# A hybrid decoder layer on one core: the gate projected as [token, channel] blocks and applied before the transposes

## The chip, the cores and the metric

One core of a Trainium2 chip runs the whole layer as one program. The metric is the device time of one execution in microseconds (us); three executions of the kernel before took 892.24, 895.63 and 896.28 us, median 895.63.

## What is computed

One decoder layer over 256 tokens of width 2048, all in float32:

```python
h    = rms_norm(x, norm_g)
proj = h @ dn_w_in                       # q 1536 | k 1536 | v 3072 | a, b 48 | xq 1024 | z 4096
mix  = deltanet_branch(...)              # causal conv + SiLU, 24 value heads of 128, gated delta rule,
                                         # each head's output through rms_norm with out_g
xa   = memory_cross_attention(xq, ...)   # 4 heads of 256 channels against 256 memory tokens
y    = concatenate([mix, xa]) * silu(z)  # 4096 channels
out  = x + y @ w_out
```

The gate is `silu(z)`, and z takes 4096 of the 11,312 columns of the input projection. The delta rule needs, for each of 24 heads and 2 chunks of 128 tokens, the inverse of a unit lower triangular 128 x 128 matrix.

## The kernel before, in words

**Weights.** All weights come as 272 units of [128, 1024] words, in the order of the list `STREAM`. `wnext` (lines 226 to 252) loads a unit on the SP queue into `st` (5 buffers), lets ScalarE cast it to a high part (line 244) and VectorE subtract for the low part (line 246); both lie in `wt` (4 buffers). Every product is three matmuls: high x high, high x low, low x high. All matmuls go through line 162 and all transposes through line 166, ordinary operations of ScalarE, VectorE and POOL through line 94; so the tiles' names tell them apart. `hkt` holds the normalised tokens, 16 tiles of [128 channels, 256 tokens], high and low.

**Two kinds of projection.** `proj_a` (lines 265 to 278) makes a tile of 128 channels x 256 tokens. The weight is stationary. For each of 16 steps there are two matmuls into one PSUM bank `pa`: the weight's high part against both parts of the tokens (512 columns), and its low part against the tokens' high part (256 columns), which is added to the second half. `halves` then adds the two halves: a ScalarE copy and a VectorE add. q, k, v, xq and z are made so. `proj_b` (lines 299 to 321) makes two tiles of 128 tokens x 512 channels at once, in two banks: tokens stationary, weights moving, three matmuls of 512 columns for each step and token half. The memory's keys and values ("K", "V") and the output projection ("o") are made so, banks by tag "A" or "pa", two of each.

**The order.** A loop at the end of `hybrid_kernel` takes one unit after another of `STREAM`: V, K and the decay inputs, 8 xq tiles, k tiles 0 to 5 with z tiles 24 to 31 between them, z tiles 0 to 11, and then twelve rounds of q, v, v, where the first two rounds also hold the other k tiles and the first six hold two z tiles each; at last the output blocks. Between units it runs side processes (generators) that are due by a cost model: `conv`, `gram`, `inverse`, `merge`, `delta`, `attend`, `decay`, `split_y`. The framework then orders instructions for each engine and sets the waits.

**The gate.** z tile pairs become `zs` [channel, token] (`silu`, 32 times 256 columns). In `delta` the output `o` [token, channel] is scaled by its norm on ScalarE (line 1054), transposed (`poT`, line 1061) and multiplied by `zs` on VectorE (line 1064). The cross-attention makes `xaT` [channel, token] directly and `gate_xa` multiplies. `split_y`, from round 9 on, splits each product into `yhi` and `ylo`, the stationary operands of the output projection.

**The inverses.** `inverse(g)`, for 12 of 24 heads each, solves the 32 x 32 diagonal blocks of 24 matrices on VectorE. It writes them transposed into the diagonal of full 128 x 128 matrices in DRAM (`dY`) and untransposed, compactly, into `dX`, both on ScalarE's queue. Then, three times, six loads fetch pieces of `dX` into `XN` and two loads fetch whole rows of `dY` into two tiles `Y`, zeros included; `merge` joins the blocks with small matmuls (`pm`). `zero_scratch` (line 787) writes the zeros of both `dY` once, on the SP queue.

Of the kernel before, what the change touches and what calls it, by code (L numbers as in the profile page):

```python
# [48 lines left out]
STREAM = [("V", 0)] * 8 + [("V", 1)] * 8 + [("K", 0)] * 8 + [("ab", 0)] + [("K", 1)] * 8  # L49


def _tiles(*ts):
    for t in ts:
        STREAM.extend([t, t])


for _t in range(8):
    _tiles(("x", _t))
for _t in range(6):
    _tiles(("k", _t), ("z", 24 + _t))  # L60
_tiles(("z", 30), ("z", 31))
for _t in range(12):
    _tiles(("z", _t))
for _t in range(NPAIR):
    _tiles(("q", _t), ("v", 2 * _t), ("v", 2 * _t + 1))
    if _t < 2:
        _tiles(*[("k", _k) for _k in ((6, 7, 8), (9, 10, 11))[_t]])
    for _i in (2 * _t + 12, 2 * _t + 13):
        if _i < 24:
            _tiles(("z", _i))  # L70
for _t in range(4):
    STREAM.extend([("o", _t)] * 16)


@with_exitstack
def hybrid_kernel(ctx: ExitStack, tc: tile.TileContext, x, xT, memT, W, prm_d, cst_d, out):
# [144 lines left out]
    wpos = [0]  # L221
# [4 lines left out]
    def wnext():  # L226
        st = stp.tile([128, 1024], F32, name="st", tag="st")
        wt = wp.tile([128, 2, 1024], F32R, name="wt", tag="wt")
        hi, lo, src = wt[:, 0, :], wt[:, 1, :], st
        if STREAM[wpos[0]][0] == "ab":  # L230

            v = wt.rearrange("p a (k c) -> p (a k c)", c=64).rearrange("p (k a c) -> p k a c", a=2, c=64)
            hi, lo, src = v[:, :, 0, :], v[:, :, 1, :], st.rearrange("p (k c) -> p k c", c=64)
        parts = 2 if wpos[0] == 0 else 1
        dma[0] = max(dma[0], free.pop(0)) + 1.46
        for a in range(parts):
            w = slice(a * 1024 // parts, (a + 1) * 1024 // parts)
            sy.dma_start(st[:, w], W[wpos[0]][:, w])
# [12 lines left out]
        free.append(ve.end)  # L251
        ahead.append((wt, ve.end))

    def wload():

        while wpos[0] < W.shape[0] and len(ahead) <= LOOK:
            wnext()
        wt, t = ahead.pop(0)
        now[0] = max(now[0], t)
        return wt  # L260
# [38 lines left out]
    def proj_b(steps, act, tag, done, before=None):  # L299
# [3 lines left out]
        for s in range(0, n, 2):  # L303
# [321 lines left out]
    xaT = [None] * 4  # L625
# [28 lines left out]
    def attend(hd, qh, ql, sq):  # L654
# [41 lines left out]
        for dt in range(2):  # L696
            c0 = (hd % 2) * 256 + dt * 128
            for m in range(2):
                exact(px[:, dt * 256 : (dt + 1) * 256], [t[:, c0 : c0 + 128] for t in vm[m][hd // 2]],
                      [t[:, m * 256 : (m + 1) * 256] for t in (pTh, pTl)], start=(m == 0), stop=(m == 1))  # L700
        yield 0.2
        xa = S2("xaT", [2, 256])
        se.copy(xa.rearrange("p a t -> p (a t)"), px)
        yield
        xaT[hd] = xa
# [70 lines left out]
    dY = [dp.tile([24, 129 * C], F32, name=f"dY{g}", tag=f"dY{g}") for g in range(2)]  # L776
# [9 lines left out]

    def zero_scratch():
        z = S2("zero", [512])
        po.memset(z, 0.0)
        for g in range(2):  # L790
            sy.dma_start(dY[g].rearrange("s e -> (s e)").rearrange("(p a e) -> p a e", p=128, a=12),
                         z[:, 0:258].unsqueeze(1).to_broadcast([128, 12, 258]))
            yield 8.0

    def inverse(g):
# [33 lines left out]
        for f in range(2):  # L829
            se.dma_start(diag(dY[g])[:, 16 * f : 16 * f + 16], xt[f])  # L830
# [3 lines left out]
        nat = dX[g].rearrange("(s k) r c -> k r s c", k=4)  # L834
        for q in range(3):
# [7 lines left out]
            ys = []  # L843
            for p2 in range(2):
                y = S2("Y", [4, C])
                s0 = 8 * q + 4 * p2
                se.dma_start(y, mat(dY[g])[s0 : s0 + 4].rearrange("s r c -> r s c"))
                ys.append(y)
            yield
            yield from merge(6 * g + 2 * q, xs, ys)  # L850
# [58 lines left out]
    zs = [None] * 16  # L909

    def z_done(j, i):
        def done(pt):
            if i == 0:
                zs[j] = S2("zs", [2, 256])
            spawn(silu(pt, j, i), 0.2)
        return done

    def silu(pt, j, i):
# [3 lines left out]
        ready.add(f"z{j}{i}")  # L922
# [3 lines left out]
    def split_y():  # L926
        for j in [12, 13, 14, 15] + list(range(NPAIR)):
            yield from until(lambda: yf[j] is not None)
            yield from calm()
            yhi[j], lo = S2("yhi", [2, 256], F32R), S2("ylo", [2, 256], F32R)  # L930
            se.copy(yhi[j], yf[j])
            yield
            ve.tensor_tensor(out=lo, in0=yf[j], in1=yhi[j], op=ALU.subtract)
            ylo[j] = lo

    def gate_xa(hd):
        yield from until(lambda: {f"z{12 + hd}0", f"z{12 + hd}1"} <= ready and xaT[hd] is not None)
        z = zs[12 + hd]
        ve.tensor_tensor(out=z, in0=xaT[hd], in1=z, op=ALU.mult)
        yf[12 + hd] = z  # L940
# [18 lines left out]
    def delta(p):  # L959
# [86 lines left out]
        yield  # L1046
        ve.scalar_tensor_tensor(out=e4[:, 1], in0=e4[:, 0], scalar=1.0 / 128,
# [7 lines left out]
        yield from pe_soon()  # L1055
        yield from until(lambda: {f"z{p}0", f"z{p}1"} <= ready)
        pt = PS("m", "poT")
        for h in range(2):
            for b in range(NB):
                w = (2 * h + b) * C  # L1060
# [31 lines left out]
    def process(kind, t):  # L1092
# [13 lines left out]
        if kind == "z":  # L1106
            return proj_a(z_done(t // 2, t % 2))
# [98 lines left out]
```

## Time and profile before

| | |
|---|---|
| profiled execution | 892.58 us, its span 890.8 us |
| TensorE matmuls, busy | 870.6 us (98%), 5331 instructions |
| VectorE, ScalarE busy | 643.3 us (72%), 565.9 us (64%) |
| DMA | 171.5 MB, mean 192 GB/s |
| mean granted TensorE clock | 0.992 of 2.4 GHz |

Times in all rows are microseconds from the span's start, unless marked ns. PE is TensorE's matmuls, PEld its weight loads, DVE VectorE, ACT ScalarE, SP the sync engine; "SPq" and "ACTq" are DMA issues on these engines' queues. A busy TensorE is not TensorE at its peak: a matmul's shown duration overlaps the next one's, so the spacing of matmuls is read from long gapless pieces.

### The profile page before, as it was taken

The page shows a single profiled execution, that of the slowest core. Times are in us where ns is not written, and L with a number is a line of the kernel's source. Part 1 is how long each engine was busy: PE and PEld are TensorE (multiplying, and loading weights), DVE is VectorE, ACT ScalarE, POOL GpSimd, SP SyncE. Part 2 cuts the span into 40 slices and gives each one's busy share as a digit, 9 for nine tenths or more (in the row PEclk, how much of TensorE's full clock was granted, in tenths as well). Part 3 has the DMA queues.
Part 4 walks back from the last instruction along what each step waited for, and adds up shares of the span by engine and source line. Part 5 has one row for each costly group of instructions (what it writes and reads, how often), then busy time and mean ns, then how long its engine had stood idle before and what let it go on. Part 6 is the DMA issues. An engine that isn't in the chain of part 4 may idle for free.

```text
span 890.8 us, 14438 instructions
## 1 busy us (share of the span) xinstructions
PE 870.6 (98%) x5331; PEld 743.9 (84%) x5331; DVE 643.3 (72%) x1267; ACT 565.9 (64%) x1046; POOL 41.9 (5%) x51
## 2 busy tenths in 40 slices
PE   7998989999999999999999999999999999999998
PEld 5886879888888888878888888888888888888886
DVE  7778777678968799867687879895688655554442
ACT  8655365587768787457667977656688656433341
POOL 0000000001000000210100000010000000000000
PEclk9998999999999999999999999999999999999999
DMA  8963885556777765776465554466354544756560
GB/s 289 346 208 124 196 269 141 166 171 216 241 207 236 232 225 173 223 205 186 153 189 189 189 187 147 148 206 201 121 178 154 170 158 159 257 192 223 192 210 24
DMA packets 82351, 171.46 MB, mean 192 GB/s; under 512 B 23760, under 2 KB 39912, under 8 KB 82280
## 3 DMA queue, kind: packets, MB, share of 16 engines
q1 hardware_dynamic: 51344, 161.25, 56.1%
q10 hardware_dynamic: 30936, 9.28, 4.3%
q8 instruction: 42, 0.69, 0.3%
q14 instruction: 29, 0.24, 0.1%
HBM read 160.50 MB, written 10.01 MB: 191 GB/s over the span
## 4 chain that ended last, share of the span: by engine, by line
PE 79%; DMA 8%; DVE 5%; issue 4%; ACT 3%; POOL 1%; ACTq 0%; SPq 0%; POOLq 0%; DVEq 0%
PE pa L162 44%; PE pb L162 26%; DMA st<-W_d 3%; PE pO L162 2%; DVE wt L246 2%; DMA dX<-inN 1%; PE pm L162 1%; DMA Y<-dY 1%; ACT wt L244 1%; PE pU L162 1%; DMA inN<-dN 1%; PE pkq L162 1%; PE xsc L162 1%; PE xo L162 1%; DVE acc L94 1%
## 5 line engine op out<-in xcount | busy, mean ns | idle before, releaser
L162 PE MATMUL pa<-hkt,wt 128*128 128x512 f32 (+1 forms) x2816 | 517.8, 341 | 3.9 <-ACT wt L244 2.0
L162 PEld LDWEIGHTS pa<-hkt,wt 128*128 128x128 f32 x2816 | 431.3, 189 | 63.4 <-DVE wt L246 2.4
L246 DVE TENSOR_TENSOR wt<-st,wt 128x1024 fp32r<-128x1024 f32 (+1 forms) x274 | 332.5, 1216 | 126.6 <-ACT wt L244 121.7
L244 ACT CAST wt<-st 128x1024 fp32r<-128x1024 f32 (+1 forms) x274 | 284.9, 1046 | 151.4 <-PE pb L162 91.3
L162 PE MATMUL pb<-wt,yhi 128*128 128x512 f32 x512 | 159.4, 392 | 0.0
L162 PEld LDWEIGHTS pb<-wt,yhi 128*128 128x128 f32 x512 | 94.8, 188 | 19.2 <-ACT yhi L94 0.3
L162 PE MATMUL pb<-wt,ylo 128*128 128x512 f32 x256 | 99.8, 390 | 0.0
L162 PE MATMUL pb<-wt,mkt 128*128 128x512 f32 x384 | 93.1, 401 | 3.6 <-ACT wt L244 2.3
L162 PEld LDWEIGHTS pb<-wt,mkt 128*128 128x128 f32 x384 | 73.7, 194 | 21.1 <-ACT wt L244 2.7
L94 DVE SCALAR_TENSOR_TENSOR acc<-raw,prm,acc 128x255 f32<-128x255 f32 x144 | 68.8, 478 | 16.2 <-ACT acc L94 15.0
L94 ACT ACT_TABLE_LOAD x43 | 55.2, 1283 | 3.3 <-DVE acc L94 1.9
L162 PEld LDWEIGHTS pb<-wt,ylo 128*128 128x128 f32 x256 | 48.1, 188 | 10.1
L94 ACT COPY raw<-pa 128x256 f32<-128x256 f32 x48 | 17.8, 372 | 29.4 <-PE pa L162 18.3
L94 DVE TENSOR_TENSOR inT<-inXT,inN 96x1 f32<-96x1 f32 (+22 forms) x92 | 29.5, 340 | 1.6 <-DMA inN<-dN 1.3
L94 ACT ACTIVATE acc<-raw,prm 128x256 f32<-128x256 f32 x48 | 24.4, 509 | 8.5 <-DMA XN<-dX 4.3
L94 DVE TENSOR_SCALAR dec<-erow,gcc 128x128 f32<-128x128 f32 x96 | 24.5, 284 | 7.2 <-DMA erow<-dgc 7.1
L94 DVE TENSOR_REDUCE inXT<-inT 96x1 f32<-96x1 f32 (+22 forms) x92 | 28.6, 335 | 0.4
L94 POOL TENSOR_TENSOR e<-e,mhalf 128x4 f32<-128x4 f32 x12 | 15.3, 1279 | 286.9 <-DVE e L94 286.9
L94 DVE TENSOR_TENSOR raw<-pa,raw 128x256 f32<-128x256 f32 x48 | 20.1, 419 | 12.0 <-ACT raw L94 11.9
L94 ACT COPY zs<-pa 128x256 f32<-128x256 f32 x32 | 11.8, 369 | 23.9 <-PE pa L162 23.9
L94 POOL TENSOR_TENSOR srk<-skt,mhalf 128x2 f32<-128x2 f32 x12 | 12.9, 1076 | 230.5 <-DVE skt L94 216.5
L94 ACT ACTIVATE o<-o,e 128x128 f32<-128x128 f32 x48 | 16.1, 395 | 5.7 <-POOL e L94 5.6
(196 smaller groups left out, 697.2 us busy)
## 6 DMA issues: line engine op xcount, KB each, us to landing
st<-W_d SPq DMA_DIRECT2D x272, 512.0 KB, 4.1
erow<-dgc SPq DMA_DIRECT2D x24, 256.0 KB, 5.0
dY<-zero SPq DMA_DIRECT2D x2, 1548.0 KB, 11.0
dN<-dec ACTq DMA_DIRECT2D x12, 256.0 KB, 2.7
Y<-dY ACTq DMA_DIRECT2D x12, 256.0 KB, 4.0
xraw<-xT_d SPq DMA_DIRECT2D x8, 256.0 KB, 5.7
res<-x_d SPq DMA_DIRECT2D x8, 256.0 KB, 4.1
mst<-memT_d SPq DMA_DIRECT2D x7, 256.0 KB, 4.9
```

What stands on the lines that cost most here:

```text
L94: return getattr(self.eng, op)(*a, **k)
L162: te.matmul(o_, lhsT, rhs, start=start, stop=stop)
L244: se.eng.copy(hi[:, w] if parts > 1 else hi, st[:, w] if parts > 1 else src)
L246: ve.eng.tensor_tensor(out=lo[:, w] if parts > 1 else lo, in0=st[:, w] if parts > 1 else src, in1=hi[:, w] if parts > 1 else hi, op=ALU.su ...
```

## The change

z is no longer made in tiles of 128 channels but in 8 blocks "Z" of 512 channels by `proj_b`; the input is laid out as before, so a Z unit is gathered from four tiles in pieces of 256 words, and the casts read it with a stride. Blocks 6 and 7 stand between k tiles 0 to 5, blocks 0 to 2 after them, and blocks 3, 4 and 5 at the ends of rounds 1, 4 and 7. The gate is multiplied in [token, channel] form, for the delta rule together with the norm's scale on VectorE, for the cross-attention after its own output has been turned round; all transposes now stand in `split_y`, which also applies the norm's gain. Within a block's first unit (as in its last before) all matmuls of the first bank come before those of the second. `dY` becomes compact like `dX`, `zero_scratch` goes, and a tile Y is zeroed by POOL and filled by four loads of its diagonal blocks.

```diff
-for _t in range(6):
-    _tiles(("k", _t), ("z", 24 + _t))
-_tiles(("z", 30), ("z", 31))
-for _t in range(12):
-    _tiles(("z", _t))
+for _t in range(6):
+    _tiles(("k", _t))
+    PLAN.extend([("Z", 6 + _t // 3)] * (3, 3, 2)[_t % 3])
+for _t in range(3):
+    PLAN.extend([("Z", _t)] * 8)
 for _t in range(NPAIR):
     _tiles(("q", _t), ("v", 2 * _t), ("v", 2 * _t + 1))
...
-    for _i in (2 * _t + 12, 2 * _t + 13):
-        if _i < 24:
-            _tiles(("z", _i))
+    if _t in (1, 4, 7):
+        PLAN.extend([("Z", 3 + _t // 3)] * 8)
...
+        if kind == "Z":
+            s4 = zpos.get(t, 0)
+            zpos[t] = s4 + 1
+            u = N_PLAIN + 8 * t
+            data = W[u : u + 8].rearrange("(t f) p c -> f p t c", f=2)[s4 // 4][:, :, s4 % 4 * 256 : s4 % 4 * 256 + 256]
+            hi, lo = [h.rearrange("p (k t c) -> p k t c", k=2, t=4) for h in (hi, lo)]
+            src = st.rearrange("p (t k c) -> p k t c", t=4, k=2)
+            dst = st.rearrange("p (t c) -> p t c", t=4)
...
-            if s + 2 == n:
+            if s == 0 or s + 2 == n:
                 rk.sort()
...
     def silu(pt, cb, r):
-        yield from halves(zs[j][:, i, :], pt)
-        se.activation(zs[j][:, i, :], zs[j][:, i, :], AF.Silu)
+        se.activation(zs[cb][r], pt, AF.Silu)
...
     def split_y():
         for j in [12, 13, 14, 15] + list(range(NPAIR)):
             yield from until(lambda: yf[j] is not None)
+            pt = PS("m", "pyT")
+            for h in range(2):
+                for b in range(NB):
+                    w = (2 * h + b) * C
+                    tr(pt[:, w : w + C], yf[j][:, b, h * C : (h + 1) * C])
+            yield 0.2
             yield from calm()
-            se.copy(yhi[j], yf[j])
-            ve.tensor_tensor(out=lo, in0=yf[j], in1=yhi[j], op=ALU.subtract)
+            if j < 12:
+                g = prm[:, P_GO : P_GO + 1]
+                se.activation(hi, pt, AF.Copy, scale=g)
+                yield
+                ve.scalar_tensor_tensor(out=lof, in0=pt, scalar=g, in1=hi, op0=ALU.mult, op1=ALU.subtract)
+            else:
+                se.copy(hi, pt)
+                yield
+                ve.tensor_tensor(out=lof, in0=pt, in1=hi, op=ALU.subtract)
...
-                se.activation(o[:, b, h, :], o[:, b, h, :], AF.Copy, scale=e4[:, 2, b, h : h + 1])
...
-                tr(pt[:, w : w + C], o[:, b, h, :])
-        ve.scalar_tensor_tensor(out=z, in0=pt, scalar=prm[:, P_GO : P_GO + 1], in1=z, op0=ALU.mult, op1=ALU.mult)
+                ve.scalar_tensor_tensor(out=o[:, b, h, :], in0=o[:, b, h, :], scalar=e4[:, 2, b, h : h + 1],
+                                        in1=zs[cb][b][:, c0 + h * C : c0 + (h + 1) * C], op0=ALU.mult, op1=ALU.mult)
...
-    dY = [dp.tile([24, 129 * C], F32, name=f"dY{g}", tag=f"dY{g}") for g in range(2)]
+    dY = [dp.tile([96, 32, 32], F32, name=f"dY{g}", tag=f"dY{g}") for g in range(2)]
...
-            se.dma_start(diag(dY[g])[:, 16 * f : 16 * f + 16], xt[f])
+            se.dma_start(dY[g][:, 16 * f : 16 * f + 16], xt[f])
...
             xs = S2("XN", [8, 64])
-            po.memset(xs, 0.0)
+            ys = [S2("Y", [4, C]) for _ in range(2)]
+            for t in [xs] + ys:
+                po.memset(t, 0.0)
...
-                se.dma_start(y, mat(dY[g])[s0 : s0 + 4].rearrange("s r c -> r s c"))
+                for k in range(4):
+                    b = slice(32 * k, 32 * k + 32)
+                    se.dma_start(ys[p2][b, :, b], tsp[k][:, s0 : s0 + 4])
...
+            return proj_b(kts, x_act, "pa" if 3 <= t < 6 else "A", z_done(t))
...
-    spawn(zero_scratch(), 90.0)
```

## Rows read from the trace of the kernel before

**Rows 1.** Page, busy us, share and instructions of each engine over the span.

```profile
PE 870.6 (98%) x5331; PEld 743.9 (84%) x5331; DVE 643.3 (72%) x1267; ACT 565.9 (64%) x1046; POOL 41.9 (5%) x51
```

**Rows 2.** Chain of waits: start, us, engine, tile, line, count; two gapless stretches.

```profile
283.95 68.17 PE pa L162 x393
...
756.45 130.34 PE pb L162 x574
```

**Rows 3.** Groups by shape: count, busy us, mean ns, idle before and releasers; `proj_a`.

```profile
L162 PEld LDWEIGHTS pa<-hkt,wt 128*128 128x128 f32 x2816 | 431.3, 189 | 63.4 <-DVE wt L246 2.4 <-ACT wt L244 2.4
L162 PE MATMUL pa<-hkt,wt 128*128 128x256 f32 x1408 | 395.3, 281 | 1.8 <-DVE wt L246 1.8
```

**Rows 4.** Timeline, 93 to 123 us: start, us, instructions, [idle before, releaser].

```profile
93.42 1.35 SPq L791 DMA_DIRECT2D dY<-zero  x2
...
109.96 2.97 PE L162 MATMUL pa<-hkt,wt 128*128 128x512 f32 x16
113.88 1.04 ACT L244 CAST wt<-st 128x1024 fp32r<-128x1024 f32 x1 [10.79 <-DMA st<-W_d]
114.98 0.50 PE L162 MATMUL pa<-hkt,wt 128*128 128x512 f32 x1 [2.05 <-ACT wt L244]
116.24 6.13 PE L162 MATMUL pa<-hkt,wt 128*128 128x256 f32 x25 [0.76 <-DVE wt L246]
```

**Rows 5.** Timeline near 436 us, the four transposes of one pair.

```profile
435.67 0.60 PE L166 MATMUL poT<-cst,o 128*128 128x128 f32 x4
```

**Rows 6.** Stretches: busy us by engine, then clock, DMA share, GB/s.

```profile
116.90:120.20 3.30, 3.30 (x12) 2.83 (x11) 2.18 (x5) 2.32 (x5) 1.01 (x1) 0.50 0.87 288
```

**Rows 7.** DMA issues of the whole run: count, KB each, median us to landing.

```profile
st<-W_d SPq DMA_DIRECT2D x272, 512.0 KB, 4.1
...
dY<-zero SPq DMA_DIRECT2D x2, 1548.0 KB, 11.0
...
dY<-inXT ACTq DMA_DIRECT2D x4, 192.0 KB, 5.9
```

**Rows 8.** Tile `XN`: loads, issue's ns min/median/max, first and last start.

```profile
L94 ACTq DMA_DIRECT2D XN<-dX x36: 309/442/1266, 377.5 to 638.1; - x36
```

**Rows 9.** Timeline of the first burst of loads for `merge`, 376 to 386 us.

```profile
376.29 0.38 ACTq L94 DMA_DIRECT2D Y<-dY  x1
...
382.68 1.04 ACT L244 CAST wt<-st 128x1024 fp32r<-128x1024 f32 x1 [3.50 <-DMA XN<-dX]
383.76 1.23 DVE L246 TENSOR_TENSOR wt<-st,wt 128x1024 fp32r<-128x1024 f32 x1 [4.12 <-DMA Y<-dY]
...
385.05 1.17 PE L162 MATMUL pa<-hkt,wt 128*128 128x512 f32 x5
```

**Rows 10.** Waits of the whole run: us in total, times, longest.

```profile
ACT wt L244 <- DMA st<-W_d: 16.8, 9, 10.8
...
PE pm L162 <- DMA Y<-dY: 2.5, 4, 1.2
```

**Rows 11.** Tile `zs`: ns min/median/max; the indented line: ACT and DVE idle until.

```profile
L94 ACT COPY zs<-pa x32: 348/372/377, 187.0 to 567.8; 128x256 f32<-128x256 f32 x32
...
L94 ACT ACTIVATE zs<-zs x32: 401/418/422, 191.2 to 570.1; 128x256 f32<-128x256 f32 x32
...
L94 DVE SCALAR_TENSOR_TENSOR zs<-poT,prm,zs x12: 736/746/751, 437.3 to 756.5; 128x512 f32<-128x512 f32 x12
...
  PE pa L162: 23.9, 22
```

**Rows 12.** Groups by shape, ScalarE.

```profile
L94 ACT ACT_TABLE_LOAD x43 | 55.2, 1283 | 3.3 <-DVE acc L94 1.9 <-issue 0.8
...
L94 ACT ACTIVATE o<-o,e 128x128 f32<-128x128 f32 x48 | 16.1, 395 | 5.7 <-POOL e L94 5.6
...
L94 ACT COPY xaT<-xo 128x512 f32<-128x512 f32 x4 | 2.3, 584 | 7.1 <-PE xo L162 7.1
```

**Rows 13.** Timeline at the start, V's second unit.

```profile
10.73 0.96 PE L162 MATMUL pb<-wt,mkt 128*128 128x512 f32 x2 [2.29 <-ACT wt L244]
```

More of the change, by code (lines that the diff above doesn't have):

```diff
@@ L67 @@
         _tiles(*[("k", _k) for _k in ((6, 7, 8), (9, 10, 11))[_t]])
-    for _i in (2 * _t + 12, 2 * _t + 13):
-        if _i < 24:
-            _tiles(("z", _i))
+    if _t in (1, 4, 7):
+        PLAN.extend([("Z", 3 + _t // 3)] * 8)
 for _t in range(4):
-    STREAM.extend([("o", _t)] * 16)
+    PLAN.extend([("o", _t)] * 16)
+STREAM = [_k for _k in PLAN if _k[0] != "Z"] + [("z", _t) for _t in range(32) for _ in range(2)]
+N_PLAIN = len(PLAN) - 64
 @with_exitstack
@@ L254, in wload @@
     def wload():
-        while wpos[0] < W.shape[0] and len(ahead) <= LOOK:
+        while wpos[0] < len(PLAN) and len(ahead) <= LOOK:
             wnext()
@@ L695, in attend @@
         px = PS("m", "xo")
[L696 to L697 removed]
+        c0 = (hd % 2) * 256
+        for r in range(2):
             for m in range(2):
[L699 to L700 removed]
+                exact(px[:, r * 256 : (r + 1) * 256], [t[:, m * 256 + r * 128 : m * 256 + (r + 1) * 128] for t in (pTh, pTl)],
+                      [t[:, c0 : c0 + 256] for t in vm[m][hd // 2]], start=(m == 0), stop=(m == 1))
         yield 0.2
[L702 removed]
+        xa = S2("xa", [2, 256])
         se.copy(xa.rearrange("p a t -> p (a t)"), px)
         yield
[L705 removed]
+        xag[hd] = xa
     def conv(pt, ct, dst, name):
@@ L908, in hybrid_kernel, with x_act, z_done, done @@
     yhi, ylo = [None] * 16, [None] * 16
[L909 to L915, printed above, removed]
-        return done
-    def silu(pt, j, i):
-        yield from halves(zs[j][:, i, :], pt)
-        se.activation(zs[j][:, i, :], zs[j][:, i, :], AF.Silu)
+    zs = [None] * 8
+    def x_act(kt, r):
+        hold(lambda: hs[kt] is not None)
+        return hs[kt][:, 0, r * 128 : (r + 1) * 128], hs[kt][:, 1, r * 128 : (r + 1) * 128]
+    def z_done(cb):
+        def done(r, pt):
+            if r == 0:
+                zs[cb] = [S2("zs", [512]) for _ in range(2)]
+            spawn(silu(pt, cb, r), 0.2)
+        return done
+    def silu(pt, cb, r):
+        se.activation(zs[cb][r], pt, AF.Silu)
         yield
-        ready.add(f"z{j}{i}")
+        ready.add(f"z{cb}{r}")
     yf = [None] * 16
@@ L928, in split_y @@
             yield from until(lambda: yf[j] is not None)
+            pt = PS("m", "pyT")
[4 more added lines that the diff above has]
+            yield 0.2
             yield from calm()
             yhi[j], lo = S2("yhi", [2, 256], F32R), S2("ylo", [2, 256], F32R)
-            se.copy(yhi[j], yf[j])
-            yield
-            ve.tensor_tensor(out=lo, in0=yf[j], in1=yhi[j], op=ALU.subtract)
+            hi, lof = [t.rearrange("e h t -> e (h t)") for t in (yhi[j], lo)]
+            if j < 12:
[3 more added lines that the diff above has]
+                ve.scalar_tensor_tensor(out=lof, in0=pt, scalar=g, in1=hi, op0=ALU.mult, op1=ALU.subtract)
+            else:
+                se.copy(hi, pt)
+                yield
+                ve.tensor_tensor(out=lof, in0=pt, in1=hi, op=ALU.subtract)
             ylo[j] = lo
     def gate_xa(hd):
[L937 to L940, printed above, removed]
+        cb = 6 + hd // 2
+        yield from until(lambda: {f"z{cb}0", f"z{cb}1"} <= ready and xag[hd] is not None)
+        xa = xag[hd]
+        for r in range(2):
+            ve.tensor_tensor(out=xa[:, r, :], in0=xa[:, r, :], in1=zs[cb][r][:, hd % 2 * 256 : hd % 2 * 256 + 256], op=ALU.mult)
+        yield
+        yf[12 + hd] = xa
     vps = [None] * NPAIR
@@ L1046, in delta @@
         yield
+        cb, c0 = p // 2, p % 2 * 256
+        yield from until(lambda: {f"z{cb}0", f"z{cb}1"} <= ready)
         ve.scalar_tensor_tensor(out=e4[:, 1], in0=e4[:, 0], scalar=1.0 / 128,
@@ L1053, in delta @@
             for h in range(2):
-                se.activation(o[:, b, h, :], o[:, b, h, :], AF.Copy, scale=e4[:, 2, b, h : h + 1])
[L1055 to L1060, printed above, removed]
-                tr(pt[:, w : w + C], o[:, b, h, :])
-        yield 0.2
-        z = zs[p].rearrange("e h t -> e (h t)")
-        ve.scalar_tensor_tensor(out=z, in0=pt, scalar=prm[:, P_GO : P_GO + 1], in1=z, op0=ALU.mult, op1=ALU.mult)
+                ve.scalar_tensor_tensor(out=o[:, b, h, :], in0=o[:, b, h, :], scalar=e4[:, 2, b, h : h + 1],
+                                        in1=zs[cb][b][:, c0 + h * C : c0 + (h + 1) * C], op0=ALU.mult, op1=ALU.mult)
         yield
-        yf[p] = zs[p]
+        yf[p] = o.rearrange("c b h e -> c b (h e)")
     order = []
```

31 lines of the change are left out of this document (12 added, 19 removed).

## The prediction

> **What bounds the kernel now.** I read the page's busy times first: TensorE is busy 98% of a span of 890.8 us [rows 1], VectorE and ScalarE far less. So I ask two things: how fast the matmuls follow each other, and where TensorE waits. The chain of waits answers the first. In the stretch that holds nothing but `proj_a` tiles, 393 records take 68.17 us, 173.5 ns each, with no gap; in the last output blocks 574 `proj_b` records take 130.34 us, 227.1 ns each [rows 2]. A `proj_a` step is a 512-wide and a 256-wide matmul, 347 ns a pair. The weight loads beside them (189 ns each) lie under the streaming [rows 3]. For the second I looked for idle time ahead of TensorE's rows. It is little: one hole near 113 us [rows 4], a few waits in front of the `merge` matmuls (`pm`), some at the start. The profiled execution took 892.58 us, 1.8 us more than its span and 3.05 us under the median of the runs shown, 895.63; the sum is made on 892.58 and the 3.05 us are put back at the end.
>
> **(a) The gate projection's own matmuls, -3.2 us.** Before, 32 tiles x 16 steps x 2 = 1024 matmuls at 173.5 ns: 177.7 us. After, 8 blocks x 16 x 2 x 3 = 768, all 512 wide, at 227.1 ns: 174.4 us. The streamed columns are the same (32 x 12,288 = 8 x 49,152); what goes is the overhead of 256 matmuls. On the path in full, as TensorE is. One record more or less in 393 is 0.45 us, so -2.7 to -3.7. The Trainium skill (TensorE: Matmul & The Clock Gate, Back-to-back issue gap) gives columns / 2.4 GHz plus 2.5 ns for a matmul alone; by that figure the estimate is 166.4 against 165.8 us, a gain of 0.6 us, and the sum would stand 2.6 us higher. The rows have 227 ns where the page has 216, and the rows decide.
>
> **(b) Transposes, +1.75 us.** The 48 of the delta rule (`poT`) move into `split_y`; the 16 of the cross-attention heads are new, as its output is now [token, channel]. Four in a row take 0.60 us from the first's start to the last's end [rows 5]; one alone would show some 0.27 us of that (the last one's latency, as the 256-wide matmuls show 281 ns at a spacing of some 347 - 227 = 120 [rows 2, 3]), so 0.33 us for three steps, 110 ns each: 16 x 0.11, about 1.75. The cross-attention's own matmuls stay 12 to a head, 256 wide.
>
> **(c) The zero fill, -4.5 us.** Two writes of 1548 KB, 11 us to landing each, are issued on SP at 93.42 us, ahead of the next weight loads [rows 4, 7]. The weight load behind them lands so late that ScalarE's cast starts after 10.79 us of idle, TensorE waits 2.05 and 0.76 us for the two halves of that weight, and then the granted clock is at half (1.2 GHz) until about 120.2 us [rows 4, 6]. From 109.96 to 122.37 us TensorE gets through 16 + 1 + 25 = 42 records; at 173.5 ns these take 7.3 us of 12.4. So 5.1 us are lost. Without the writes the load lands as others do (4.1 us [rows 7]) and the hole closes. What is late next: K's second block ends just there, and its squares, its rsqrt on POOL and its transposes would meet a TensorE that comes 5 us sooner. I keep 0.6 us for that; bounds -2.8 (the idle alone) and -5.1.
>
> **(d) The inverses' way through DRAM, +1.0 us.** One load of Y becomes four, 8 instead of 2 in each of six bursts, all on ScalarE's queue behind six XN loads: 36 issues more. An issue of this form takes 0.44 us there [rows 8], so each burst holds ScalarE, casts included, 6 x 0.44 = 2.65 us longer, less what the smaller transfers give back. What is queued behind: the next weight's cast. In the first burst it started at 382.68 us after waiting for an XN load, its residual ended at 384.98, and TensorE used it at 385.05 [rows 9]: no cover there. TensorE waits for Y itself 2.5 us in four places [rows 10]. Against that, the writes of the diagonal blocks become contiguous (now 5.9 us to landing [rows 7], rows of 32 words), and the first burst of either group waits for just these writes: up to 2.5 us back, twice. The order on the engines is not the source's (of the first burst one Y load, at 376.29 us, stands ahead of the first XN load, at 377.5 [rows 8, 9]), so the scheduler will place the merges later if it expects longer loads. Bounds: -2.5 (the present Y waits go) and +8 (2.65 us in three bursts without cover). I take +1.0, nearer the lower end: of the twelve Y loads only four made TensorE wait, so several bursts do end ahead of the matmuls that need them.
>
> **(e) Handing over PSUM banks, +1.8 us.** A `proj_a` tile leaves its bank while another tile streams for 5.5 us. Blocks 7, 0, 1, 2 follow one another on the two "A" banks, and blocks 3 to 5 take both "pa" banks: 12 hand-overs. With the new order of a block's first and last unit a bank has six matmuls, 1.36 us, less the drain of 0.16, to be read. One Silu of 256 columns takes 418 ns; a copy of 512 takes 0.21 us more than one of 256 (584 against 372) [rows 11, 12], so 0.63 us: 0.57 to spare. ScalarE stood ready and waiting in 22 of 32 cases [rows 11]; in the others a cast (1.04 us [rows 9]) or a table load (1.28 us [rows 12]) is in front. A third of the hand-overs losing 0.4 to 0.5 us makes 1.8; bounds 0 and 5.
>
> **(f) The rest, +0.6 us.** `split_y` now holds an "m" bank over transposes, a scaled copy and a subtraction, for 13 tiles that are ready at once when it starts, while `delta` needs the same two banks: 0 to +3. The last pair's way loses one VectorE step (746 ns [rows 11]): 0 to -1.3. Costed at nothing: weight loads in 1 KB pieces (loads hold casts up 16.8 us in the run, 10.8 of it the hole of (c) [rows 10], so they land early); the new order in V's first unit (TensorE then waits until 10.73 us for the second unit anyway [rows 13]; if that cover went, three matmuls, 0.7 us). Off the path: 32 copies (372 ns), 32 adds and 32 Silus (418 ns [rows 11]) become 16 Silus of 0.63 us, 15 us less on ScalarE; the scaling of o (48 x 395 ns, 16.1 us busy [rows 12]) goes from ScalarE to VectorE.
>
> Sum: -3.2 + 1.75 - 4.5 + 1.0 + 1.8 + 0.6 = -2.55 us. 892.58 - 2.55 = 890.0 for a profiled execution, 893.1 against the median.
>
> **Rivals.**
> - Clean gain. No hand-over waits, the fast writes pay for the added issues, all 5.1 us come back: -3.2 + 1.75 - 5.1 - 1.5 = -8.0 us, 887.6. For it: 22 of 32 evictions were on time, and ScalarE and VectorE lose work. Against it: leads in the merge stretches are near nothing.
> - Slower: ScalarE's queue. Every burst holds casts and evictions 2.65 us longer and TensorE pays in all six, 16 us, with the hand-overs at their upper end half way (+3.5): -6.0 + 16 + 3.5, about +13 us, 909. It decides for a loss as soon as over two of the six bursts have no cover (2.2 x 2.65 = 5.8). For it: the first burst has none. Against it: ScalarE has about 30 us less other work, and the schedule knows of the loads.
> - Bank hand-overs: (e) at its upper end, 3.2 us more, and the "m" banks of (f) at theirs, 2.4 us more: -2.55 + 5.6 = +3.05, 898.7. For it: 10 of 32 evictions found ScalarE busy. Against it: the work it would be busy with gets less.
> - The zero fill was not the cause, only the bystander of a late load: (c) is nought, +1.95 us, 897.6. Against it: DMA is issued in order and the loads are behind 3 MB.
> - Weight loads are exposed. If each of the 256 loads saved were paid in full, 189 ns [rows 3], the gate would gain 48.4 us instead of 3.2: 847.9. The Trainium skill (TensorE: Matmul & The Clock Gate, The mechanism) states that a load overlaps running matmuls only when its row group differs, and here all fill the array. The trace is against it: 227 ns from matmul to matmul leaves no room for 189 ns beside 512 columns at 2.4 GHz.
>
> **How the numbers follow.** Forecast (within some 3 us of 893.1) 0.47; clean gain 0.29; ScalarE's queue 0.12; upper hand-overs 0.07; bystander 0.04; exposed loads 0.01. A measurement of this kernel tells about 0.5%, 4.5 us, from no change: faster means under 891.1, slower over 900.1. The forecast lies within, with a part of it (0.04) below; clean gain is faster bar a part (0.02). So faster 0.29 - 0.02 + 0.04 + 0.01 = 0.32, slower 0.12 + 0.03 (of the upper hand-overs) = 0.15, same 0.53. The range, 8 in 10, goes from 885 (clean gain with the runs' own scatter of some 2 us) to 902 (three bursts without cover).
>
> **What the profile after would show.** (a) gate blocks at about 227 ns a matmul, 21.8 us a block; (b) 64 transposes into one tile of `split_y`; (c) no idle near 113 us and no half clock behind it; (d) the waits of `pm` for Y: under 2.5 us in all for the clean gain, over 6 for the queue; (e) TensorE waiting for ScalarE's Silu where a block starts. I am wrong if a stretch without these parts changes its length, above all the delta chain at the end, or if Z's loads in 1 KB pieces hold up casts.

## The result, and the profile after

The changed kernel takes 890.32 us (median of 8 runs, 888.07 to 891.0); the kernel before, run beside it, 894.38 (8 runs, 892.24 to 896.28). The ratio is 0.9946, with a 95% interval from 0.9931 to 0.9962: 0.5% faster, on the edge of what a measurement of this kernel can tell from no change. The forecast was 893.1 with a range from 885 to 902. The profiled execution took 890.17 us, against 892.58 of the one of before: 2.4 us less, where the sum had said 2.55 less.

The page's busy times of the changed kernel (same columns as [rows 1]): TensorE is still the bound, with 240 instructions fewer; ScalarE is busy 41 us less.

```profile
PE 870.1 (98%) x5091; PEld 732.1 (82%) x5091; DVE 636.3 (72%) x1275; ACT 524.8 (59%) x936; POOL 45.9 (5%) x62
```

The chain of waits of the changed kernel (start, us, what; it answers to [rows 2]):

```profile
110.07 7.41 PE pa L166 x42
131.19 9.19 PE pa L166 x52
...
300.29 22.08 PE pb L166 x96
...
744.26 140.15 PE pb L166 x618
```

The first line is the place of the hole: 42 records in 7.41 us, where [rows 4] had 42 in 12.4. The piece that starts at 131.19 us is 4.88 us sooner than in the chain of before (below). The third line is gate work in its new form, 230 ns a matmul. The last one is the output projection, which runs into the end: 574 records in [rows 2], 618 now, as one gap of 0.7 us that used to stand ahead of them, at the last pair's transposes, is gone.

The kernel before, the same piece of its chain, which no row ahead shows:

```profile
136.07 9.20 PE pa L162 x52
```

The stretch of the hole, 93 to 123 us, in the changed kernel (busy us of PE, PEld, DVE, ACT, POOL, then clock, DMA share, GB/s), to be read beside the half clock of [rows 6]: TensorE busy throughout, at full clock.

```profile
93.00:123.00 30.00, 30.00 (x152) 25.39 (x151) 26.93 (x44) 16.29 (x29) 1.12 (x1) 1.00 0.61 195
```

TensorE's waits over the run (us in total, times, longest), which answer to [rows 10]:

```profile
PE pb L166 <- ACT zs L98: 2.2, 3, 1.5
PE pb L166 <- ACT wt L261: 1.9, 2, 1.3
PE pyT L170 <- DVE ylo L98: 1.9, 2, 1.1
PE pab L166 <- DVE hkt L98: 1.8, 1, 1.8
PE pb L166 <- DVE wt L263: 1.5, 3, 0.7
PE pa L166 <- DVE wt L263: 1.3, 1, 1.3
```

The four waits of `pm` for Y, 2.5 us [rows 10], are gone. New are a gate block that waits for the Silu of the block that held its bank (`zs`), and `split_y` waiting for its "m" bank (`pyT<-ylo`). Matmuls that wait for a weight's cast or residual (`wt`) are not new: 4.7 us in these rows, 6.4 us in the kernel before, of which 2.8 were the hole [rows 4].

The DMA issues (count, KB each, median us to landing; `dY<-inXT` took 5.9 us before [rows 7], and a Y 4.0):

```profile
dY<-inXT ACTq DMA_DIRECT2D x4, 192.0 KB, 2.8
Y<-dY ACTq DMA_DIRECT2D x48, 16.0 KB, 1.8
```

And the transposes in the tile `pyT` (ns min/median/max, first and last start), 64 where [rows 5] stand for 48:

```profile
L170 PE MATMUL pyT<-cst,o x48: 270/272/308, 645.2 to 744.0; 128*128 128x128 f32 x48
L170 PE MATMUL pyT<-cst,xa x16: 270/272/273, 631.4 to 638.6; 128*128 128x128 f32 x16
```

Where the 2.4 us went can be added up from the matmul records. Take for each matmul the time to the next one's start, less what that form takes in a gapless stretch (227 ns for `proj_b`, 231 and 117 for the two of `proj_a`, 109, 25 and 10 for widths of 128, 64 and 32). What is over is lost time, waits and half clock alike. A cell stands for one execution: in the first row `dy_alone` and `zl_4` run, up to 90 us, what the kernel before runs, and differ from it by 1.5 us (their clock is at half for 3.4 us near 83 us, its clock for 6.9), so a difference of that size in one cell shows nothing by itself. By stage, in us, for the profiled executions of all kernels that the next section needs:

| stage (us) | before | changed | gate_alone | gate_zl | gate_zl_tags | tags | zero_later | dy_alone | zl_4 | gate_zl_4 |
|---|---|---|---|---|---|---|---|---|---|---|
| to 100 | 14.5 | 14.5 | 13.5 | 14.3 | 14.0 | 14.4 | 13.9 | 13.0 | 13.0 | 13.4 |
| 100-130, the hole | 5.0 | 0.5 | 4.6 | 0.5 | 0.5 | 0.3 | 0.5 | 0.4 | 0.5 | 0.5 |
| 130-240 | 2.8 | 2.8 | 3.1 | 2.8 | 2.8 | 2.8 | 2.7 | 2.7 | 2.5 | 2.8 |
| 240-360, gate blocks | 0.9 | 4.6 | 4.8 | 5.8 | 1.3 | 1.1 | 3.6 | 0.7 | 1.3 | 4.7 |
| 360-470, first merges | 9.0 | 9.0 | 6.5 | 7.6 | 9.3 | 10.5 | 8.9 | 16.9 | 23.6 | 17.0 |
| 470-560 | 1.7 | 1.3 | 1.4 | 1.4 | 1.4 | 1.3 | 2.1 | 1.3 | 0.9 | 1.7 |
| 560-690, second merges | 7.5 | 10.0 | 7.2 | 7.1 | 8.2 | 9.9 | 7.5 | 9.9 | 17.3 | 15.5 |
| 690 to end | 2.1 | 0.7 | 2.2 | 2.2 | 2.2 | 0.7 | 2.1 | 1.1 | 2.5 | 1.0 |
| lost in all | 43.5 | 43.4 | 43.3 | 41.7 | 39.7 | 41.0 | 41.3 | 46.0 | 61.6 | 56.6 |
| matmuls as such | 841.7 | 839.6 | 839.6 | 839.6 | 839.6 | 839.6 | 841.7 | 841.7 | 841.7 | 839.6 |

So in the profiled executions the change takes 2.1 us of matmuls away (the gate's, less 16 transposes), takes 4.5 us from the hole, and loses nearly all of the latter again: 3.7 us in the gate blocks and 2.5 in the second merges, less 1.8 that come back from 470 to 560 us and at the end.

### The profile page after: what moved, and what is told of

Its sections match the earlier page's. It is cut to its first block, busy times and chain, and to the rows that moved or that the text cites. A ratio compares the mean times of both kernels' runs of the same rounds, so it can differ in the third digit from the quotient of the medians.

```text
span 888.4 us, 13971 instructions
## 1 busy us (share of the span) xinstructions
PE 870.1 (98%) x5091; PEld 732.1 (82%) x5091; DVE 636.3 (72%) x1275; ACT 524.8 (59%) x936; POOL 45.9 (5%) x62
## 4 chain that ended last, share of the span: by engine, by line
PE 81%; DVE 6%; DMA 4%; ACT 3%; issue 3%; POOL 1%; ACTq 1%; SPq 0%; DVEq 0%; POOLq 0%
PE pb L166 43%; PE pa L166 29%; PE pO L166 2%; DVE wt L263 2%; DMA st<-W_d 2%; PE pm L166 1%; ACT wt L261 1%; PE pU L166 1%; PE pkq L166 1%; DVE acc L98 1%; PE xsc L166 1%; DMA erow<-dgc 1%; DMA XN<-dX 1%; PE xo L166 1%; PE pyT L170 1%
## 5 line engine op out<-in xcount | busy, mean ns | idle before, releaser
L166 PE MATMUL pa<-hkt,wt 128*128 128x512 f32 (+1 forms) x1792 | 336.5, 342 | 1.5 <-DVE wt L263 1.3
L166 PEld LDWEIGHTS pa<-hkt,wt 128*128 128x128 f32 x1792 | 274.1, 188 | 40.0 <-DVE wt L263 1.4
L166 PE MATMUL pb<-wt,hkt 128*128 128x512 f32 x768 | 183.9, 394 | 4.3 <-ACT zs L98 2.2
L166 PEld LDWEIGHTS pb<-wt,hkt 128*128 128x128 f32 x768 | 141.5, 188 | 35.4 <-ACT zs L98 3.5
L98 POOL TENSOR_TENSOR e<-e,mhalf 128x4 f32<-128x4 f32 x12 | 13.5, 1123 | 270.9 <-DVE e L98 270.9
L98 POOL TENSOR_TENSOR srk<-skt,mhalf 128x2 f32<-128x2 f32 x12 | 12.4, 1032 | 221.4 <-DVE skt L98 221.4
```

Source lines behind the costliest of these rows:

```text
L98: return getattr(self.eng, op)(*a, **k)
L166: te.matmul(o_, lhsT, rhs, start=start, stop=stop)
```

## The experiments

Ratios are to the kernel before, run on the same chip beside the kernel; 0.001 is 0.9 us. By the intervals a difference of two ratios is uncertain by 0.002 to 0.004, some 2 to 3.5 us.

**One half of the change each.** `gate_alone` is the changed kernel with the old 128x128 scratch, its zero fill and one load per Y; `dy_alone` is the kernel before with the compact scratch.

```
 # dy_alone, to the kernel before
-dY = [dp.tile([24, 129 * C], ...)]        -spawn(zero_scratch(), 90.0)
+dY = [dp.tile([96, 32, 32], ...)]
-    se.dma_start(y, mat(dY[g])[s0 : s0 + 4].rearrange("s r c -> r s c"))
+    for k in range(4):
+        b = slice(32 * k, 32 * k + 32)
+        se.dma_start(ys[p2][b, :, b], tsp[k][:, s0 : s0 + 4])
```

> The gate part alone (blocks of 512, gate ahead of the transposes); the full DRAM scratch, its zero fill and the single loads of Y stay as before. Theory A (the gain is the zero fill's; the gate's own 3.2 us less 1.75 us of transposes are eaten by waits at the hand-over of PSUM banks and in front of the transposes): 0 to +3 us against before, ratio 1.000 to 1.0035, and the hole near 113 us is there, some 5 us. Theory B (the gain is the gate's): ratio 0.994 to 0.997.

> The DRAM part alone: compact scratch, no zero fill, four loads for each Y, 36 issues more on ScalarE's queue; the gate as before. Theory A: the hole's 4.9 us, and up to 1 us of Y waits: -5 to -6 us, ratio 0.9935 to 0.9945. Theory B: no change, ratio 0.998 to 1.002. The rival of ScalarE's queue: the added issues cost up to 2.65 us in a burst, ratio 0.996 or above with the hole closed.

Measured: `gate_alone` 0.9986 (0.9971 to 1.0001), `dy_alone` 1.0043 (1.0026 to 1.006). The first lies between the ranges of its two theories, nearer to theory A's, the second is what its rival foresaw. Together the halves would be 0.3% slower, and the whole is 0.5% faster: they do not add up. `gate_alone` still has the hole, with the same weight load in the chain of waits:

```profile
93.85 18.71 DMA st<-W_d
```

and the half clock behind it (stretch, busy us by engine, clock, DMA share, GB/s):

```profile
93.00:123.00 30.00, 27.39 (x129) 22.71 (x128) 22.88 (x38) 12.83 (x24) 1.01 (x1) 0.94 0.98 263
```

`dy_alone` has lost the hole (0.4 us in the table), as expected, and then loses 7.9 us more than before in the first merges and 2.4 in the second. Its timeline of ScalarE and ScalarE's queue (ACTq) in the first burst (start, us, count):

```profile
367.83 4.08 ACTq L94 DMA_DIRECT2D XN<-dX  x6
...
372.47 0.37 ACT L94 COPY raw<-pa 128x256 f32<-128x256 f32 x1 [4.30 <-DMA XN<-dX]
372.79 4.06 ACTq L94 DMA_DIRECT2D Y<-dY  x7
376.89 1.04 ACT L244 CAST wt<-st 128x1024 fp32r<-128x1024 f32 x1 [4.04 <-DMA Y<-dY]
```

Its largest wait of TensorE:

```profile
PE pa L162 <- DVE wt L246: 4.3, 3, 3.1
```

And its stretches (busy us of PE, PEld, DVE, ACT, POOL, then clock, DMA share, GB/s):

```profile
368.00:377.00 9.00, 8.52 (x51) 7.24 (x50) 2.05 (x10) 0.65 (x3) 0.68 (x1) 1.00 0.60 183
377.00:380.00 3.00, 2.01 (x39) 1.53 (x40) 2.03 (x4) 3.00 (x4) 0.00 (x0) 0.99 0.07 11
380.00:383.40 3.40, 3.40 (x57) 2.66 (x55) 3.27 (x10) 1.93 (x5) 2.21 (x3) 0.50 0.51 167
444.90:448.20 3.30, 3.12 (x10) 2.73 (x11) 2.73 (x10) 2.60 (x7) 1.01 (x1) 0.50 0.48 159
```

From 368 to 377 us ScalarE does 0.65 us of work: it issues DMAs. The next weight's cast comes at 376.89, TensorE waits 1.5 us for it, until 377.99, and from 380 us on the clock is at half for 3.4 us. That is the rival "ScalarE's queue", in the half of the change that was to bring the gain. The largest wait of the first merges comes later: until 441.32 us VectorE is idle for 3.1 us before a step of the second inverse that needs a load (`inN`), a weight's residual stands behind that step, TensorE waits 3.1 us until 445.08, and the clock is at half for 3.3 us from 444.9 on. That the additional issues made this load late is argued, not tested.

**The zero fill alone.** `zero_later` is the kernel before with the fill cut in twelve, one piece every 6 us from 130 us on by the cost model's clock; in the trace the pieces are issued from 126.9 to 146.3 us.

```
-    sy.dma_start(dY[g]...[128, 12, 258]); yield 8.0        # x2, from 90 us
+    for a in range(0, 12, 2):
+        sy.dma_start(dY[g]...[:, a : a + 2], z[...][128, 2, 258]); yield 6.0
```

> Before, with the same zero fill made in twelve pieces of 258 KB, one every 6 us by the schedule's clock from 130 us on, instead of two of 1548 KB at 90 us. Nothing else changes. Theory A: the hole at 113 us closes and no other opens: -4.9 us, ratio 0.9945. If the zero fill were a bystander of a late load: ratio 1.000 and the hole stays.

Measured: 0.9959 (0.9944 to 0.9974). The same bytes are written, and the hole is gone; the chain reaches the piece that started at 136.07 us in the kernel before at

```profile
130.61 9.19 PE pa L162 x52
```

The pieces themselves, among the DMA issues:

```profile
dY<-zero SPq DMA_DIRECT2D x12, 258.0 KB, 7.2
```

So the fill's place and size together made the hole, and nothing of it needs a smaller scratch. Not all of its 4.5 us show in the time (3.7 us by the ratio). In the profiled execution 2.7 are lost again between 240 and 360 us: TensorE waits 1.6 us until 263.52 where the kernel before waits 1.1, and the gapless piece behind that wait runs at 177 ns a matmul, against 173.5 in [rows 2]. Why the same matmuls follow each other more slowly there is open.

```profile
263.52 92.25 PE pa L162 x521
```

**Bank hand-overs.** `tags` is the changed kernel with the gate blocks' bank pairs chosen so that blocks that follow one another do not share one.

```
-return proj_b(kts, x_act, "pa" if 3 <= t < 6 else "A", z_done(t))
+return proj_b(kts, x_act, "A" if t in (1, 6, 7) else "pa", z_done(t))
```

> After, with the banks of blocks 0 and 2 changed from A to pa, so that blocks 7, 0, 1, 2 alternate. Theory A (hand-overs cost about 2.7 us between those blocks): TensorE's waits for the Silus of zs between blocks go, -2 to -2.7 us against after, ratio 0.9917 to 0.9925 against before. Rival (ScalarE is late there anyway and the wait moves to the casts): ratio 0.9946, as after.

Measured: 0.9924 (0.9908 to 0.9939). The wait of `pb` for `zs` is gone, and the chain has one piece for what was broken into many:

```profile
259.54 55.79 PE pb L166 x246
```

246 records in 55.79 us are 226.8 ns each: the gate's price without hand-overs. By the table 3.5 us go from the gate blocks, and 1.5 of them come back in the first merges: a wait of 1.5 us for a cast, until 397.92 us, is followed there by 3.4 us at half clock.

**Which part of the compact scratch costs.** Four kernels: `gate_zl` is `gate_alone` with `zero_later`'s fill, `gate_zl_tags` adds the bank pairs of `tags`; `zl_4` and `gate_zl_4` are `zero_later` and `gate_zl` with each Y loaded in four DMAs of 32 rows, as many issues as the compact scratch has, from the old scratch.

```
 # zl_4 and gate_zl_4
-    se.dma_start(y, mat(dY[g])[s0 : s0 + 4].rearrange("s r c -> r s c"))
+    for k in range(4):
+        b = slice(32 * k, 32 * k + 32)
+        se.dma_start(y[b], mat(dY[g])[s0 : s0 + 4].rearrange("s r c -> r s c")[b])
```

> The gate part of the change, with the old 128x128 scratch for the inverses and its zero fill cut into twelve pieces of 258 KB from 130 us on. Theory A (the compact scratch costs the changed kernel next to nothing, its gain is the missing hole near 113 us): this kernel stands where the changed kernel does, ratio 0.993 to 0.9965 to the kernel before, no hole, the matmul records from 110 to 131 us as dense as in the changed kernel. Theory B (the profiled spans of gate_alone and the changed kernel, 888.2 and 888.4 us with and without a 3.5 us hole, say that the compact scratch gives 3 us back in the merges): this one is about 3 us faster than the changed kernel, ratio 0.990 to 0.992.

> gate_zl with the Z blocks' bank pairs chosen so that no two blocks in a row share one (pair A for blocks 1, 6 and 7, pair pa for the others). Theory A (compact scratch neutral; bank hand-overs worth 2 us or more, as in tags): ratio 0.9905 to 0.993. Theory B (the compact scratch costs 3 us): 0.987 to 0.990.

> zero_later with every Y loaded in four DMAs of 32 rows instead of one of 128: 36 more DMA issues on ScalarE's queue, nothing else of the compact scratch. Theory A (dy_alone lost its 5 to 8 us because the additional issues hold ScalarE's queue, 7 of them in a row, 3.9 us, ahead of a weight's cast): ratio at or above 1.000 against zero_later's 0.996, with a TensorE wait for a wt behind the Y loads of the first burst. Theory B (dy_alone's loss comes from elsewhere: where the second inverse starts, or the merges themselves): 0.995 to 0.998, as zero_later.

> gate_zl with every Y loaded in four DMAs of 32 rows: the same 36 additional issues on ScalarE's queue as in zl_4, but in the weight order of the changed kernel. Theory A (the order decides: in the new order the bursts fall where gate blocks in [token, channel] form are running, which need 2 casts where the old order needs more, so the queue's 16 us of issues cost little): 0.9935 to 0.998, at most 4 us over gate_zl's 0.9933. Theory B (the issues cost the same wherever they fall; the compact scratch is cheap in the changed kernel because its stores land sooner and its loads are 64 KB in 128 B rows): 1.012 to 1.018, 18 to 21 us over gate_zl, as zl_4 stands to zero_later.

Measured: `gate_zl` 0.9933 (0.9907 to 0.9958), `gate_zl_tags` 0.9912 (0.989 to 0.9934), `zl_4` 1.0207 (1.0182 to 1.0232), `gate_zl_4` 1.0099 (1.007 to 1.0127). The first two came as their theory A had it, and `zl_4` is beyond the 1.000 of its own; `gate_zl_4` lies between its two ranges, nearer to theory B. With the others they make a table of the way through DRAM, all without the hole:

| weight order | 12 loads, old scratch | 48 loads, old scratch | 48 loads, compact scratch |
|---|---|---|---|
| before | 0.9959 (`zero_later`) | 1.0207 (`zl_4`) | 1.0043 (`dy_alone`) |
| changed | 0.9933 (`gate_zl`) | 1.0099 (`gate_zl_4`) | 0.9946 (changed kernel) |

The 36 issues cost 22 us in the order of before and 15 in the changed one; the smaller scratch gives 15 and 14 of these back. Their net is 7.5 us in the one order and 1.2 in the other, the latter well inside the intervals. My first theory, that the new order shelters the issues, does not hold: there too they cost 15 us by themselves. The 36 issues without the smaller transfers show how the price arises. Stretches of `zl_4`, then of `gate_zl_4` (columns as above):

```profile
380.00:387.00 7.00, 6.37 (x87) 4.92 (x88) 5.67 (x9) 5.01 (x10) 0.00 (x0) 0.53 0.61 188
431.00:438.00 7.00, 6.03 (x44) 5.24 (x41) 6.02 (x18) 5.20 (x11) 0.69 (x1) 0.54 0.29 94
656.00:663.00 7.00, 5.47 (x55) 4.58 (x45) 4.50 (x8) 6.68 (x19) 0.00 (x0) 0.56 0.22 75
```

```profile
450.00:460.00 10.00, 10.00 (x116) 7.60 (x116) 7.45 (x17) 6.64 (x16) 0.00 (x0) 0.51 0.53 171
586.00:593.00 7.00, 5.91 (x88) 4.53 (x88) 6.19 (x12) 4.93 (x9) 0.00 (x0) 0.55 0.30 90
```

TensorE's waits in these stretches are not the wait for a `wt` that I had expected behind the Y loads, or not alone: it waits for Y itself as well, which is whole only when the last of its four loads has landed (us in total, times, longest; `zl_4`, then `gate_zl_4`):

```profile
PE pm L162 <- DMA Y<-dY: 2.0, 2, 1.1
PE pm L166 <- DMA Y<-dY: 3.2, 5, 1.2
```

The longest of these in `gate_zl_4`, until 449.30 us, stands ahead of its 10 us at half clock. Behind waits of 0.7 to 3.1 us the granted clock is at its lower level, 1.2 GHz, for 3 to 10 us, in the merges as in the hole. A late load or cast is paid once as a wait and a second time as half clock, and the second can be the larger part: from 360 to 690 us TensorE is idle for 11.0 us in `zl_4` and for 4.3 in `zero_later`, while the clock of `zl_4` is at half for 24 us there, which can cost up to 12 (an estimate: half of 24), and that of `zero_later` never. The changed kernel waits at the same place, 1.3 us until 401.16 us, behind this row of issues,

```profile
397.36 2.26 ACTq L98 DMA_DIRECT2D Y<-dY  x5
399.66 0.51 ACT L98 ACTIVATE acc<-raw,prm 128x256 f32<-128x256 f32 x1 [3.78 <-DMA Y<-dY]
400.08 2.92 ACT L261 CAST wt<-st 128x1024 fp32r<-128x1024 f32 x3
```

and its clock stays up: in the profiled execution it has no half clock between 89 us and the last microsecond. What it is in the smaller scratch that saves the 14 us is left open. In the order of before the writes land in 3.1 us (`dy_alone`) instead of 5.4 (`zl_4`), and a Y load, 16 KB instead of 64, in 1.7 instead of 2.1; in the changed order it is 2.8 us instead of 3.2 (`gate_zl_4`) and 1.8 instead of 2.3. So in the latter the writes hardly differ and 14 us are saved all the same; no run takes writes and loads apart.

**The transposes.** `tr2` is the changed kernel with each of the 64 transposes of `split_y` issued twice (`for _ in range(2): tr(...)`).

> The changed kernel with each of the 64 gated-output transposes issued twice. Theory A (TensorE is the bound there, so a transpose costs its slot of 110 ns): 64 x 110 ns = 7.0 us more than the changed kernel, ratio 1.001 to 1.004. Theory B (the transposes stand in time in which TensorE would wait for its second operand's split anyway): under 2 us more, ratio 0.994 to 0.997.

Measured: 1.0021 (1.0007 to 1.0034), 0.0075 over the changed kernel: 6.7 us for 64, 105 ns each (75 to 135 by the intervals). They are on the path. The two profiled executions are only 3.5 us apart; that of `tr2` lacks, among others, the changed kernel's two waits of `pyT`.

**Two tries at the rest.** `split6` starts `split_y` at pair 6 (`SPLIT = ("q", 6)`); `zcont` lays the gate's weights out as 128x1024 blocks, so that its loads are rows of 4 KB instead of pieces of 1 KB.

> The changed kernel with the splits of the gated output started at pair 6 instead of pair 9, so that the ten or so batches of transposes queued at pair 9 are spread. Theory A (TensorE's two waits for a bank of pair m, 1.9 us, and the stall of 1.3 us at 644 us come from that batch): 1 to 2.5 us faster than the changed kernel, ratio 0.992 to 0.9937. Theory B (pair m is then shared with the second merge burst, 570 to 640 us, and the waits move there): 0.9945 to 0.998.

> The changed kernel with the gate's weights laid out in DRAM as 128x1024 blocks, so that its 64 loads are rows of 4 KB instead of four pieces of 1 KB, and the cast reads and writes in one order. Theory A (the loads are hidden behind TensorE, the casts at 1.05 us too): the same as the changed kernel, 0.993 to 0.9962. Theory B (the 1 KB pieces hold the weight stream up where the loads are late): 1.5 us or more faster, 0.9925 or less.

`split6`: 0.9989 (0.997 to 1.0007), slower than the changed kernel; the median is above both ranges, though the interval reaches into theory B's. Its transposes and splits now meet the second merges, where ScalarE issues eight loads of Y in a row (timeline of ScalarE and its queue):

```profile
587.50 4.97 ACTq L98 DMA_DIRECT2D Y<-dY  x8
592.52 0.69 ACT L98 ACTIVATE yhi<-pyT,prm 128x512 fp32r<-128x512 f32 x1 [5.33 <-DMA Y<-dY]
```

TensorE waits 0.8 and 0.6 us for Y there and 0.4 for a cast, with a stretch at half clock behind:

```profile
594.60:601.30 6.70, 6.70 (x35) 4.27 (x38) 6.05 (x8) 3.92 (x7) 0.00 (x0) 0.50 0.56 157
```

`zcont`: 0.9921 (0.9896 to 0.9946), 0.0025 under the changed kernel, though the intervals overlap and no row shows a wait of that size. To tell, `best` puts it on top of `gate_zl_tags`.

> gate_zl_tags and zcont together: the gate in the changed kernel's form with its weights as 128x1024 blocks in DRAM and with bank pairs that alternate, the old scratch for the inverses with the zero fill in twelve late pieces. Theory A (zcont's 2.2 us against the changed kernel were real, a saving in the loads): 0.987 to 0.990. Theory B (they were the spread between batches, no trace shows a wait of that size): 0.990 to 0.993, as gate_zl_tags.

Measured: 0.9914 (0.9888 to 0.994), where `gate_zl_tags` had 0.9912. On top of `gate_zl_tags` the layout of the gate's weights in DRAM brings nothing; whether it does in the changed kernel, with its hand-overs, these two runs leave open. `gate_zl_tags`, at 884.22 us, is 0.9% under the kernel before, and its ratio is 0.0034 under the changed one's, with intervals that just overlap: the gate in its new form with alternating banks, the old scratch, its fill in late pieces.

## Why the prediction came out as it did

**The total.** 890.0 was the sum for a profiled execution, and it took 890.17. The 2.8 us between the forecast, 893.1, and the median, 890.32, come from the step that added 3.05 us for the profiled execution of before standing under its median. It was a low one among its own runs (892.58 of 892.24 to 896.28), that of the changed kernel stood at its median, and a median of three was too little to carry such an offset over. That the sum itself met the profiled execution to 0.2 us is in part luck: as (d) and (f) show, it was reached with terms of which several were far too small or had another cause, and which cancelled.

**(a) Gate matmuls: right.** Forecast -3.2, from 227.1 ns. Measured 226.8 ns without hand-overs: 768 x 226.8 = 174.2 us against 177.7, -3.5. The Trainium skill's figure (TensorE: Matmul & The Clock Gate, Back-to-back issue gap) would have given -0.6; its 216 ns for 512 columns, stated for a matmul alone, are not what these rows show. Its rule on weight loads (the same page, The mechanism), the rival of 847.9 us, is refuted here: the weight loads of 189 ns lie under matmuls that follow each other every 227 ns, and 256 loads fewer gave a few us, not 48.

**(b) Transposes: right.** 110 ns each forecast, 105 measured by doubling them, with the spread given above.

**(c) The zero fill: right.** Forecast -4.5. The profile has -4.88 at 131 us; `zero_later` gives -3.7 in the times, `gate_zl` against `gate_alone` -4.7. The 0.6 us kept for what is late next did not show: TensorE's wait for the keys' transposes stayed at 1.2 us (1.1 before). What `zero_later` lost again it lost later, at 240 to 360 us, where the prediction had nothing. The bystander rival (897.6) falls with `zero_later`.

**(d) The way through DRAM: net right by luck, both of its parts wrong.** Forecast +1.0, measured +1.2, from `gate_zl` to the changed kernel, with 2.7 either way by the intervals. But the issues were priced as time on ScalarE's queue, 2.65 us a burst, 16 us if every burst paid. That time is there: the 84 issues of XN and Y in the changed kernel add up to 37.5 us, the 48 of before to 21.6, 15.9 more. But it is not what is paid: in `zl_4` TensorE's idle time in the merges grows by 6.7 us (4.3 to 11.0), less than half of it, and with the half clock behind the waits the whole comes to 22 us. The half clock was in no term of (d). Against it I had set up to 2.5 us twice for faster transfers; the runs show 14 to 15, what is spared of the half clock with it. Two terms, each several times too small, met at the right difference. In the order of before the same edit costs 7.5 us, near my upper bound of 8. The rival with ScalarE's queue, 16 us for the issues and a chance of 0.12, did not come in the changed kernel; `zl_4` and `gate_zl_4` show that its size was real, 22 and 15 us. I had set against it that the schedule knows of the loads. The kernel's own cost model, by which the side processes become due, knows them at 0.06 us an issue (`se_cost`, in both kernels), where the trace has 0.44 [rows 8]; no run changed this number.

**(e) Bank hand-overs: right.** Forecast +1.8. `tags` takes 2.0 us off the changed kernel, and `gate_zl_tags` 1.9 off `gate_zl`. Each of the two differences is about as large as its uncertainty; the profiles bear them out. In the profiled execution they cost more (3.7 us in the table's gate blocks), still under the bound of 5; what `tags` saves of that is partly lost in the first merges. Few hand-overs pay, but those much: the longest wait for `zs` is 1.5 us, where I had four of 0.4 to 0.5. So the rival with the hand-overs at their upper end (898.7) did not come, and they are also what the clean gain (887.6) counted at nothing.

**(f) The rest: the size right, the causes wrong.** Forecast +0.6, from the "m" banks (0 to +3) and the last pair's shorter way (0 to -1.3). The changed kernel has a loss and a gain of that kind: two waits of `pyT`, 1.9 us, and 1.4 us less from 690 us to the end. But neither comes from the gate's new form alone. `gate_alone` and `gate_zl` have the same `split_y` and the same last step; they wait 0 and 0.4 us for `ylo`, lose 2.2 us at the end where the kernel before loses 2.1, and wait in front of the last transposes as it does (the kernel before, then `gate_alone`):

```profile
PE poT L166 <- ACT o L94: 0.5, 1, 0.5
PE pyT L170 <- DVE o L98: 0.6, 1, 0.6
```

`dy_alone`, which has the gate of before, hasn't got that wait and loses 1.1 us at the end (`zl_4` hasn't got it either, but loses 2.5 elsewhere in that stage). So the shorter end goes with the four loads of a Y, which move the merges and all that follows, and a gain from the last pair's shorter way isn't shown. How the loads do it is open, and so is why the waits of `pyT` come with the compact scratch; both are contained in the +1.2 us of (d). The prediction had named a changed length of the delta chain at the end, without a part of its own in it, as a sign that it is wrong: in this term it was. `split6` shows that the batch isn't to be had cheaper by starting sooner. The loads in 1 KB pieces land later, 5.2 us against 4.6 in `zcont` (median, 245 to 305 us), but cost nothing that `best` shows.

**A term that was missing.** The gate's part of the sum, (a), (b), (e) and (f), is +0.95 us; `gate_alone` is 1.3 us faster than before (interval from 2.6 faster to none), `gate_zl` 2.3 faster than `zero_later`, with 2.6 either way. By the table it is in the first merges, 9.0 against 6.5 and 8.9 against 7.6: with 12 loads as before, the bursts now fall elsewhere in the weight stream, and `pm` waits 0.6 us for Y in `gate_alone` (1.0 in `gate_zl`) instead of 2.5 [rows 10]. I had let the gate's new order leave the merges alone. The gain isn't firm: `gate_zl_tags` loses 9.3 us there, with 3.4 us at half clock from 398 us on. In the changed kernel the additional issues take it again.

## To carry to other kernels

A DMA issue on a compute engine's queue is paid by whatever stands behind it there, and by the last load of the row itself; where TensorE waits for either, price the wait and the half clock that may follow it, and find out by adding the issues alone. If the kernel times its work by a cost model, see what that model books for an issue. Two halves of a change that move the same bursts need not add up, as here, so price each half in the order in which it will run. A large write in one piece ahead of a just-in-time load can be spread out before anything is redesigned to avoid it.

## What the runs showed of the hardware

- The clock is the second price of a short wait. In `dy_alone` TensorE stood idle for 1.5 of 12 us (8.52 us busy of 9 from 368 us on, 2.01 of 3 from 377), and then ran at 1.2 GHz for 3.4 us; in `gate_zl_4` 10 us in a row were at that level, behind a wait of 1.25 us. A wait of 1.3 us in the changed kernel, until 401.16 us, was followed by none, one of 1.5 us at the same place in `tags` by 3.4 us at half clock: which waits bring the clock down wasn't settled.
- 3 MB written in two pieces delayed the weight load behind them (18.71 us in `gate_alone`'s chain, where loads take 4.1 [rows 7]); with the same 3 MB in twelve pieces, 7.2 us to landing each, from 126.9 to 146.3 us, TensorE waited for nothing until 262 us (`zero_later`).
- On ScalarE's queue an issue of a Y load took 0.44 us (median of 48 in the changed kernel), whether the load carried 16 KB or 64 (`zl_4`, 0.44), and in `dy_alone` ScalarE did nothing else during seven of them, from 372.84 to 376.85 us.
- Weight loads of 512 KB from pieces of 1 KB landed 0.6 us later than from rows of 4 KB (medians of 20 or 21 loads from 245 to 305 us: 5.2 and 4.6 us in the changed kernel and `zcont`, 5.4 and 4.8 in `gate_zl_tags` and `best`); the time was the same in the latter two (0.9912 and 0.9914).
